# Attention in groups of four heads with one two-bank score tile, in a float32 decoder on one core

## The chip, the cores and the metric

The kernel runs on one core of one Trainium2 chip. The metric is the device time of one execution in microseconds. Three runs of the kernel before took 1315.48, 1319.79 and 1320.84 us; the median is 1319.79 us.

## The reference

A sequence of 256 tokens of width 1024 goes through two decoder layers and then through one layer of another kind. A decoder layer is a feed-forward block, a mixer and another feed-forward block. The mixer projects the normalized tokens and runs four attentions side by side, each of 256 columns, whose outputs are joined and multiplied by `w_out`:

```python
ya = neighbourhood_mixer(...)   # 4 heads of 64, additive bias per head
yb = mla_mixer(...)             # 4 heads of 96 (64 + 32 with rope), no bias
yc = diff_mixer(...)            # 4 heads, two maps of 32 each, additive bias
yd = gqa_mixer(...)             # 4 query heads of 64 on 2 key heads, no bias
x = x + jnp.concatenate([ya, yb, yc, yd], axis=-1) @ w_out[l]

# dense attention, per block of 128 queries
logits = einsum('bqhd,bkhd->bhqk', q, k) * scale (+ bias)
p = softmax(logits); y = einsum('bhqk,bkhd->bqhd', p, v)
# differential attention: two maps m per head, one value
p = softmax(logits)                       # b h m q k
w = p[:, :, 0] - lam * p[:, :, 1]
```

The last layer has 8 heads of causal attention over the 256 tokens (`moba`), 8 heads of causal attention in a window of 128 with a sink logit in the softmax (`swa`), a pooling branch, and gates. All weights and activations are float32.

## The kernel before, in words

TensorE (PE) is given every product twice or three times: each weight is staged from memory (`st`), rounded on ScalarE to `hi` and its rest `lo` formed on VectorE (`Weights.cut`, a unit of 1024 columns each), and `acc` (L339) issues three matmuls of 128 rows by up to 512 columns for one 128-row piece of it. These are the rows `mmps<-...` of the trace; the text calls them the weight matmuls. `proj` (L496) and `wide` (L521) loop over them. After each piece they call `tick` (L446), which runs pieces of other work that a small time model (`Clock`) takes to be ready: norms, rope, and the attentions, each written as a generator. So the attentions are dealt out between the weight matmuls, in an order that is fixed when the program is built. Each engine then works off its own queue in order.

An attention hands `softmax_pv` (L572) a list of jobs. Before the change a job is one block of 128 queries with two heads, or one differential head with its two maps. It has four steps:

- `scores` (L581): the products of queries and keys, for the two halves s = 0 and 1 of the job, into two score tiles of 256 columns in PSUM (`psS`, L321, trace name `sps`, one buffer each, each in a bank of its own). Where a bias is added VectorE writes score plus bias to `E` and takes its maximum in one instruction (trace name CUSTOM_DVE_ANT_0); else it takes the maximum alone (TENSOR_REDUCE, `nm<-sps`). ScalarE takes the exponential of each half with its sum (`E`). A differential job then combines its two maps on VectorE (`E<-E,cf`).
- `transposes` (L628): PE transposes `E` (128 by 128 each) into a tile `tps`, and ScalarE copies it to `PT`.
- `values` (L638): PE multiplies the values with `PT`. The outputs of the two halves lie in rows 0 to 63 and 64 to 127 of one `tps` tile; a differential job has one half only. ScalarE copies to `yt`.
- `finish` (L657): PE transposes `yt`, VectorE scales by the reciprocal of the sum into `y`. After the last job of a query block `post` norms and transposes `y` into `yT`, which `wide` needs for `w_out`.

The loop at the end of `softmax_pv` (L684 to L703) starts the scores of a job while up to two score steps are ahead of the transposes (`i1 - i2 < 2`), and allows two `PT` at once. There are 8 differential jobs and 4 of each other attention in a layer, and 8 each of `moba` and `swa`: 56 in all. `tps` has two buffers (L242) and serves all transposes of the kernel, `mmps` has four (L240).

The tags in `wk` have two buffers unless said otherwise, so there are two `E` tiles and two `PT` tiles.

Of the kernel before, what the change touches and what calls it, by code (L numbers as in the profile page):

```python
# [10 lines left out]
F = mybir.dt.float32  # L11
# [218 lines left out]
def decoder(ctx, tc, a, out):  # L230
# [10 lines left out]
    s_p = [pool(f"s{i}", 1, space=PSUM) for i in range(2)]  # L241
# [56 lines left out]

    def v3(ap, n):
        return ap.rearrange("p (k n) -> p k n", n=n)  # L300
# [20 lines left out]
    def psS(i):  # L321
        ps = s_p[i].tile([128, 256], F, tag="s", name="sps")
        clock.ring(f"s{i}", 1, ps)
        return ps
# [247 lines left out]
    def softmax_pv(jobs, post, scored=None, have_v=lambda: True):  # L572
# [3 lines left out]
        n = len(jobs)  # L576
        diff = "nlam" in jobs[0]
        ns = 1 if diff else 2
        E, PT, YT, yts = {}, {}, {}, {}

        def scores(i):  # L581
            jb = jobs[i]
            w = jb["nk"] * 128
            ps = [psS(s) for s in range(2)]
            e = E[i] = wk.tile([128, 2, 256], F, tag="E", name="E")
            for s in range(2):
                q, k = jb["qk"][s]
                if not isinstance(q, tuple):
                    mm(ps[s][:, :w], q, k, True, True)
                    continue  # L590
                mm(ps[s][:, :w], q[0], k[0], True, False)
                mm(ps[s][:, :w], q[0], k[1], False, False)
                mm(ps[s][:, :w], q[1], k[0], False, True)
            nm = stat.tile([128, 2], F, tag="nm", name="nm")
            if jb["bias"] is not None:
                mx = stat.tile([128, 2], F, tag="mx", name="mx")
                for s in range(2):
                    dve.tensor_tensor_reduce(
                        out=e[:, s, :w], in0=ps[s][:, :w], in1=jb["bias"][s], scale=1.0,
                        scalar=-3e38, op0=ALU.add, op1=ALU.max, accum_out=mx[:, s:s + 1])  # L600
                dve.tensor_scalar(nm, mx, -1.0, None, op0=ALU.mult)
                src = [e[:, s, :w] for s in range(2)]
            else:
                src = [ps[s][:, :w] for s in range(2)]
# [3 lines left out]
            if "nsink" in jb:  # L608
                dve.tensor_tensor(out=nm, in0=nm, in1=jb["nsink"], op=ALU.min)
                es = stat.tile([128, 2], F, tag="es", name="es")  # L610
                dve.tensor_tensor(out=es, in0=nm, in1=jb["nsink"], op=ALU.subtract)
                act.activation(out=es, in_=es, func=ACTF.Exp)
            sm = stat.tile([128, 2], F, tag="sm", name="sm")
            for s in range(2):
                act.activation(out=e[:, s, :w], in_=src[s], func=ACTF.Exp, bias=nm[:, s:s + 1],
                               accum_out=sm[:, s:s + 1])
            if "nsink" in jb:
                dve.tensor_tensor(out=sm, in0=sm, in1=es, op=ALU.add)
            rs = jb["rs"] = stat.tile([128, 2], F, tag="rs", name="rs", bufs=6)
            dve.reciprocal(out=rs, in_=sm)  # L620
            if diff:
                cf = stat.tile([128, 1], F, tag="cf", name="cf")
                dve.scalar_tensor_tensor(out=cf, in0=sm[:, 0:1], scalar=jb["nlam"],
                                         in1=rs[:, 1:2], op0=ALU.mult, op1=ALU.mult)
                dve.scalar_tensor_tensor(out=e[:, 0, :], in0=e[:, 1, :], scalar=cf,
                                         in1=e[:, 0, :], op0=ALU.mult, op1=ALU.add)

        def transposes(i):  # L628
            nk = jobs[i]["nk"]
            ps = psT().rearrange("p (s k q) -> p s k q", s=2, k=2)  # L630
            PT[i] = wk.tile([128, 2, 2, 128], F, tag="PT", name="PT")
            for s in range(ns):
                for k in range(nk):
                    T(ps[:, s, k, :], E[i][:, s, tok(k)])
            copy(0, PT[i][:, :ns, :nk, :], ps[:, :ns, :nk, :])
            del E[i]

        def values(i):  # L638
            jb = jobs[i]
            ps = psT()[:, :128]  # L640
            for s in range(ns):
                r = slice(64 * s, 64 * s + 64)
                for k in range(jb["nk"]):
                    mm(ps[r, :], jb["v"][s][k], PT[i][:, s, k, :], k == 0, k == jb["nk"] - 1)
            if diff and i % 2 == 0:
                yts[0] = wk.tile([128, 128], F, tag="yt", name="yt")
            elif not diff:
                yts[0] = wk.tile([128, 128], F, tag="yt", name="yt")
# [8 lines left out]
        def finish(i):  # L657
            if diff and i % 2 == 0:
                return
# [52 lines left out]
    def mixers(l, cols, rows, nlam, norm_out):  # L712
# [337 lines left out]
        w = []  # L1050
# [393 lines left out]
```

## Time and profile before

| | |
|---|---|
| median of three runs | 1319.79 us |
| the profiled execution | 1318.63 us |
| its span, first to last instruction | 1316.5 us |
| PE busy | 1291.3 us (98%) |
| VectorE (DVE) busy | 792.7 us (60%) |
| ScalarE (ACT) busy | 722.5 us (55%) |
| mean granted clock of PE | 0.995 |

Times in the trace count from the start of the span. The first layer's attentions lie at about 226 to 330 us, the second's at 747 to 850, those of the last layer at 1089 to 1163. A row of a PE timeline merges neighbouring instructions of one kind; matmuls overlap in their rows, so what a step takes from PE is read from its start to the start of the next row, not from its own duration. A float32 matmul shows as two rows, so "x4" for values in the trace is "x2" in the program's order.

### The profile page before, as it was taken

How to read it: one execution, taken by the hardware profiler on the slowest of the kernel's cores; microseconds unless marked ns; L12 is line 12 of the kernel's file. 1: busy time of each engine (PE TensorE's matmuls, PEld its weight loads, DVE VectorE, ACT ScalarE, POOL GpSimd, SP SyncE). 2: the span in 40 equal slices, each digit the busy share in tenths (PEclk: the TensorE clock that was granted, in tenths of full speed). 3: DMA queues.
4: the chain of work that ended last, by engine and by line, in shares of the span. 5: the costliest groups of instructions: out<-in, count | busy, mean ns of one | idle time of the engine just before them, and what ended most of it. 6: DMA issues, size and time to landing. Idle time of an engine off the chain costs nothing.

```text
span 1316.5 us, 17826 instructions
## 1 busy us (share of the span) xinstructions
PE 1291.3 (98%) x6514; PEld 1046.1 (79%) x6514; DVE 792.7 (60%) x1615; ACT 722.5 (55%) x1223; POOL 28.6 (2%) x44
## 2 busy tenths in 40 slices
PE   8999999999999999999999999999999999999997
PEld 7788888766788888788888876678888887678886
DVE  5655449895655544755545798565554565555475
ACT  6544437866644444644435676664444466566543
POOL 0000001000000000100000000000000000000000
PEclk9999999999999999999999998999999999999999
DMA  8766657432566665666665733156667474245652
GB/s 278 219 181 188 183 166 238 126 97 65 172 190 184 183 188 164 208 183 188 186 186 167 218 115 98 45 179 189 185 181 235 144 234 127 80 145 168 205 170 80
DMA packets 109815, 221.80 MB, mean 168 GB/s; under 512 B 7456, under 2 KB 30368, under 8 KB 109728
## 3 DMA queue, kind: packets, MB, share of 16 engines
q1 hardware_dynamic: 109152, 220.04, 55.5%
q8 instruction: 51, 0.84, 0.3%
q10 hardware_dynamic: 576, 0.63, 0.1%
q14 instruction: 36, 0.29, 0.1%
HBM read 219.59 MB, written 1.05 MB: 168 GB/s over the span
## 4 chain that ended last, share of the span: by engine, by line
PE 82%; DMA 6%; DVE 5%; ACT 4%; issue 1%; POOL 1%; SPq 0%; POOLq 0%; ACTq 0%; DVEq 0%
PE mmps L333 71%; PE tps L337 6%; PE sps L333 3%; DMA st<-in_w_in_dram 3%; PE tps L333 3%; DVE lo L154 2%; ACT hi L154 2%; DMA st<-in_ffn_w_gate_dram 2%; DMA st<-in_ffn_w_up_dram 1%; DVE xTl L153 1%; ACT junk L154 1%; ACT xTh L153 1%; POOL r L154 1%; DVE x L153 0%; DVE qkT L153 0%
## 5 line engine op out<-in xcount | busy, mean ns | idle before, releaser
L154 DVE TENSOR_TENSOR lo<-st,hi 128x1024 fp32r<-128x1024 f32 (+2 forms) x403 | 488.2, 1214 | 395.3 <-ACT hi L154 394.5
L154 ACT ACTIVATE hi<-st 128x1024 fp32r<-128x1024 f32 (+2 forms) x403 | 421.9, 1050 | 427.6 <-PE mmps L333 348.8
L333 PE MATMUL mmps<-hi,xTh 128*128 128x512 f32 (+2 forms) x1200 | 451.9, 377 | 1.0 <-ACT xTh L153 1.0
L333 PE MATMUL mmps<-hi,xTl 128*128 128x512 f32 (+2 forms) x1200 | 446.3, 372 | 0.0
L333 PE MATMUL mmps<-lo,xTh 128*128 128x512 f32 (+2 forms) x1200 | 446.2, 372 | 0.0
L333 PEld LDWEIGHTS mmps<-hi,xTh 128*128 128x128 f32 x1200 | 226.1, 188 | 42.4 <-issue 2.5
L333 PEld LDWEIGHTS mmps<-hi,xTl 128*128 128x128 f32 x1200 | 226.2, 188 | 38.2 <-issue 0.5
L333 PEld LDWEIGHTS mmps<-lo,xTh 128*128 128x128 f32 x1200 | 226.3, 189 | 36.2 <-issue 1.0
L333 PE MATMUL mmps<-lo,hTh 128*128 128x512 f32 x352 | 138.1, 392 | 0.0
L333 PE MATMUL mmps<-hi,hTh 128*128 128x512 f32 x352 | 137.8, 392 | 0.0
L333 PE MATMUL mmps<-hi,hTl 128*128 128x512 f32 x352 | 113.6, 389 | 0.0
L333 PE MATMUL mmps<-hi,yT 128*128 128x512 f32 (+1 forms) x248 | 89.0, 416 | 0.6 <-ACT yT L153 0.6
L333 PEld LDWEIGHTS mmps<-hi,hTl 128*128 128x128 f32 x352 | 66.1, 188 | 13.6
L333 PEld LDWEIGHTS mmps<-hi,hTh 128*128 128x128 f32 x352 | 66.1, 188 | 13.6
L333 PEld LDWEIGHTS mmps<-lo,hTh 128*128 128x128 f32 x352 | 66.1, 188 | 13.1
L154 POOL TENSOR_TENSOR r<-ms,mhalf 128x1 f32<-128x1 f32 x40 | 28.4, 711 | 1283.1 <-DVE ms L154 1283.0
L333 PEld LDWEIGHTS mmps<-hi,yT 128*128 128x128 f32 x248 | 46.1, 190 | 11.4 <-ACT yT L153 1.9
L333 PE MATMUL mmps<-lo,yT 128*128 128x512 f32 (+1 forms) x124 | 49.7, 401 | 0.0
L154 ACT ACTIVATE E<-E,nm 128x256 f32<-128x256 f32 (+1 forms) x80 | 38.3, 480 | 14.9 <-DVE nm L154 14.7
L153 ACT ACTIVATE fg<-mmps,r 128x512 f32<-128x512 f32 (+1 forms) x48 | 31.1, 652 | 21.7 <-PE mmps L333 21.7
L153 ACT ACTIVATE xTh<-tps,gains 128x128 fp32r<-128x128 f32 x112 | 31.6, 365 | 15.5 <-PE tps L337 15.5
L153 ACT ACTIVATE PT<-tps 128x512 f32<-128x512 f32 (+1 forms) x56 | 27.9, 502 | 21.4 <-PE tps L337 20.8
(172 smaller groups left out, 1035.0 us busy)
## 6 DMA issues: line engine op xcount, KB each, us to landing
st<-in_w_in_dram SPq DMA_DIRECT2D x90, 512.0 KB, 4.0
st<-in_ffn_w_up_dram SPq DMA_DIRECT2D x88, 512.0 KB, 4.0
st<-in_ffn_w_down_dram SPq DMA_DIRECT2D x88, 512.0 KB, 3.6
st<-in_ffn_w_gate_dram SPq DMA_DIRECT2D x87, 512.0 KB, 3.8
st<-in_w_out_dram SPq DMA_DIRECT2D x24, 512.0 KB, 3.7
st<-in_w_in_dram SPq DMA_DIRECT2D x8, 416.0 KB, 4.2
scratch<-in_t5b_dram SPq DMA_DIRECT2D x4, 512.0 KB, 5.1
scratch<-in_nab_dram SPq DMA_DIRECT2D x4, 512.0 KB, 7.3
```

The costliest lines, as they stand in the source:

```text
L153: return f(*args, **kw)
L154: return f(*args, **kw)
L333: nc.tensor.matmul(ps, lhsT=lhsT, rhs=rhs, start=start, stop=stop)
L337: nc.tensor.transpose(ps, src, ident)
```

## The change

A job becomes a group: four heads of one query block, as two pairs p = 0 and 1 of two halves s; for the differential attention two heads with both maps. There are 28 groups in place of 56 jobs. `psS` gives one tile of two banks, half s in bank s; the whole tile is one buffer. A group has two `E` tiles. Maxima of attentions without a bias are taken over both pairs at once, the small statistics have four columns, and a differential group multiplies the transposes of its two heads with their values into the two row halves of one tile. `PT` of the second pair is copied by VectorE. The loop lets a group's scores start only once the transposes of the group ahead have been issued (`i1 == i2`), and one group's `PT` at a time. Below is its core.

```diff
-    s_p = [pool(f"s{i}", 1, space=PSUM) for i in range(2)]
+    s_p = pool("s", 1, space=PSUM)
...
-        ps = s_p[i].tile([128, 256], F, tag="s", name="sps")
-        clock.ring(f"s{i}", 1, ps)
+        ps = s_p.tile([128, 2, 2, 256], F, tag="s", name="sps")
+        clock.ring("s", 1, ps)
...
         def scores(i):
...
+            ps = psS()
+            es = E[i] = [wk.tile([128, 2, 256], F, tag="E", name="E") for _ in range(2)]
+            for p in range(2):
                 for s in range(2):
...
+                    q, k = g["qk"][p][s]
+                    o = ps[:, s, p, :w]
...
+                    mm(o, q[0], k[0], True, False)
+                    mm(o, q[0], k[1], False, False)
+                    mm(o, q[1], k[0], False, True)
...
                 for s in range(2):
-                    dve.tensor_reduce(out=nm[:, s:s + 1], in_=src[s], axis=AX.X, op=ALU.max,
-                                      negate=True)
+                    dve.tensor_reduce(out=two(nm)[:, :, s], in_=ps[:, s, :, :w], axis=AX.X,
+                                      op=ALU.max, negate=True)
...
         def transposes(i):
...
+            if diff:
+                ps = psT().rearrange("p (s k q) -> p s k q", s=2, k=2)
+                pt = wk.tile([128, 2, 2, 128], F, tag="PT", name="PT")
+                for p in range(2):
+                    for k in range(nk):
+                        T(ps[:, p, k, :], E[i][p][:, 0, tok(k)])
+                copy(0, pt, ps)
+                PT[i] = [pt]
+            else:
+                for p in range(2):
...
+                    for s in range(2):
+                        for k in range(nk):
+                            T(ps[:, s, k, :], E[i][p][:, s, tok(k)])
+                    copy(p, pt[:, :, :nk, :], ps[:, :, :nk, :])
+                    PT[i].append(pt)
...
         def values(i):
...
+            w = 128 if diff else 256
+            ps = psT()[:, :w]
+            for p, pt in enumerate(PT[i]):
+                for s in range(2):
+                    v = g["v"][s] if diff else g["v"][p][s]
+                    for k in range(g["nk"]):
+                        mm(ps[64 * s:64 * s + 64, tok(p)], v[k], pt[:, s, k, :], k == 0,
+                           k == g["nk"] - 1)
...
-            elif i2 < i1 and att["pt"] < 2 and e_at[i2] <= now:
+            elif i2 < i1 and att["pt"] < 1 and e_at[i2] <= now:
...
-            elif i1 < n and i1 - i2 < 2 and (i1 == 0 or e_at[i1 - 1] <= now + 300):
+            elif i1 < n and i1 == i2:
...
             for t in range(2):
-                for h in range(4):
-                    rs = [slice(64 * (h % 2) + 32 * m, 64 * (h % 2) + 32 * m + 32)
-                          for m in range(2)]
+                for j in range(2):
+                    rs = [slice(64 * j + 32 * m, 64 * j + 32 * m + 32) for m in range(2)]
```

How this moves instructions is read from the order of the two built programs. Line 333 of the kernel before, where all matmuls are issued, is line 337 after, and the transposes' L337 is L341.

First, PE in the differential attention of layer 0, before: steps of one head (`sps` are scores, `tps<-ident,E` transposes, `tps<-PT,v` values) among the weight matmuls.

```order
L337 MATMUL tps<-ident,E 128x128 x2
L333 MATMUL sps<-qkT 128x256 x6
L333 MATMUL mmps<-hi,xTh 128x512
L333 MATMUL tps<-PT,v 64x128 x2
L333 MATMUL mmps<-lo,xTh 128x512
L333 MATMUL mmps<-hi,xTl 128x512
L337 MATMUL tps<-ident,yt 128x128
```

The same place after, with steps of two heads.

```order
L337 MATMUL sps<-qkT 128x256 x12
L337 MATMUL mmps<-hi,xTh 128x512
L341 MATMUL tps<-ident,E 128x128 x4
L337 MATMUL mmps<-lo,xTh 128x512
L337 MATMUL mmps<-hi,xTl 128x512
L337 MATMUL mmps<-hi,yT 128x384
L337 MATMUL mmps<-lo,yT 128x384
L337 MATMUL mmps<-hi,yT 128x384
L337 MATMUL tps<-PT,v 64x128 x4
```

Twelve score matmuls and four value matmuls stand in a row where six and two did; the weight matmuls between are the same in number over the attention.

Second, PE where the latent attention (`kT,qT` of 96 rows) begins in layer 0, before.

```order
L337 MATMUL tps<-ident,u 128x128 x8
L333 MATMUL sps<-kT,qT 128x256 x2
L333 MATMUL mmps<-hi,yT 128x512
L333 MATMUL sps<-kT,qT 128x256
L337 MATMUL tps<-ident,E 128x128 x2
L333 MATMUL sps<-kT,qT 128x256
L337 MATMUL tps<-ident,E 128x128 x2
L333 MATMUL sps<-kT,qT 128x256 x2
```

The same place after: the scores of the first group, then those of the second.

```order
L337 MATMUL sps<-kT,qT 128x256 x4
L337 MATMUL mmps<-hi,yT 128x512 x2
L337 MATMUL sps<-kT,qT 128x256 x2
L341 MATMUL tps<-ident,yn 128x128 x2
L341 MATMUL tps<-ident,u 128x128 x4
L337 MATMUL sps<-kT,qT 128x256
L337 MATMUL mmps<-hi,yT 128x512
```

And a little later after, from the values of the first group on into the neighbourhood attention (`qkT`).

```order
L337 MATMUL mmps<-hi,yT 128x512 x2
L337 MATMUL tps<-PT,v 64x128 x8
L341 MATMUL tps<-ident,E 128x128 x8
L337 MATMUL sps<-qkT 128x256 x3
L341 MATMUL tps<-ident,yt 128x128 x2
L337 MATMUL sps<-qkT 128x256 x9
L337 MATMUL tps<-PT,v 64x128 x8
L337 MATMUL sps<-qkT 128x256 x6
L341 MATMUL tps<-ident,E 128x128 x2
L337 MATMUL sps<-qkT 128x256 x2
L341 MATMUL tps<-ident,E 128x128 x2
L337 MATMUL sps<-qkT 128x256 x2
```

ScalarE's queue of that place after, from the exponentials of the first latent group to those of the second.

```order
L153 ACTIVATE E,sm<-sps,nm 128x256 x4
L153 ACTIVATE yT<-tps,gcol 128x2x128
L153 ACTIVATE qkT<-tps,qcol 128x2x128
L153 ACTIVATE qkT<-tps 128x2x128
L154 ACTIVATE hi<-st 128x1024
L153 ACTIVATE qkT<-tps,qcol 128x2x128
L153 ACTIVATE PT<-tps 128x512
L153 ACTIVATE qkT<-tps 128x2x128
L154 ACTIVATE hi<-st 128x1024
L153 ACTIVATE yt<-tps 128x256
L153 ACTIVATE E,sm<-sps,nm 128x256 x4
```

The second group's exponentials have moved behind the first group's `yt`, and its transposes stand directly behind the first group's values, with no weight matmul between.

Third, PE in the grouped-query attention of layer 0, before (scores `kT,qT`, values `PT,ug`).

```order
L333 MATMUL sps<-kT,qT 128x256 x3
L337 MATMUL tps<-ident,E 128x128 x2
L333 MATMUL mmps<-hi,yT 128x512
L333 MATMUL sps<-kT,qT 128x256 x3
L337 MATMUL tps<-ident,E 128x128 x2
L333 MATMUL mmps<-lo,yT 128x512
L333 MATMUL mmps<-hi,yT 128x512 x2
```

The same place after.

```order
L337 MATMUL sps<-kT,qT 128x256 x11
L341 MATMUL tps<-ident,E 128x128 x8
L337 MATMUL sps<-kT,qT 128x256 x3
L341 MATMUL tps<-ident,yn 128x128 x2
L337 MATMUL sps<-kT,qT 128x256 x3
L337 MATMUL tps<-PT,ug 64x128 x8
L337 MATMUL sps<-kT,qT 128x256 x6
L341 MATMUL tps<-ident,yt 128x128 x2
```

The transposes of a group stand directly behind its own scores, and no weight matmul lies between there and the group's output transposes.

## Rows read from the trace of the kernel before

**Rows 1.** The page: PE over the span, and its granted clock by slices.

```profile
PE 1291.3 (98%) x6514; PEld 1046.1 (79%) x6514; DVE 792.7 (60%) x1615; ACT 722.5 (55%) x1223; POOL 28.6 (2%) x44
...
PEclk9999999999999999999999998999999999999999
```

**Rows 2.** The page: shares of the chain of work that ended last.

```profile
PE 82%; DMA 6%; DVE 5%; ACT 4%; issue 1%; POOL 1%; SPq 0%; POOLq 0%; ACTq 0%; DVEq 0%
```

**Rows 3.** Stretches: us, busy time (instructions) of each engine, clock, DMA share, GB/s.

```profile
core 0: us, PE busy (x) PEld busy (x) DVE busy (x) ACT busy (x) POOL busy (x), PEclk, DMA share, GB/s
226.40:279.70 53.30, 52.77 (x308) 40.73 (x308) 45.54 (x178) 40.51 (x97) 2.10 (x2) 1.00 0.50 149
279.70:329.60 49.90, 47.06 (x296) 32.46 (x295) 34.30 (x148) 32.90 (x101) 2.74 (x5) 0.97 0.17 50
...
799.90:850.50 50.60, 47.63 (x291) 32.94 (x290) 34.31 (x147) 32.51 (x101) 2.74 (x5) 0.93 0.16 47
...
1088.70:1162.90 74.20, 74.00 (x456) 52.01 (x457) 39.98 (x155) 47.33 (x131) 0.00 (x0) 1.00 0.32 93
```

**Rows 4.** Timeline of PE, differential attention: start us, us, instruction.

```profile
248.11 0.40 PE L333 MATMUL mmps<-hi,xTl 128*128 128x512 f32 x1
248.44 0.65 PE L333 MATMUL tps<-PT,v 128*64 128x128 f32 x4
249.02 0.62 PE L333 MATMUL sps<-qkT 32*128 32x256 f32 x6
249.57 0.50 PE L333 MATMUL mmps<-hi,xTh 128*128 128x512 f32 x1
249.91 0.40 PE L333 MATMUL mmps<-lo,xTh 128*128 128x512 f32 x1
250.15 0.40 PE L333 MATMUL mmps<-hi,xTl 128*128 128x512 f32 x1
```

**Rows 5.** Timeline of PE: values of two heads, both row halves.

```profile
288.99 0.67 PE L333 MATMUL tps<-PT,v 128*64 128x128 f32 x8
289.58 0.50 PE L333 MATMUL mmps<-hi,yT 128*128 128x512 f32 x1
```

**Rows 6.** Timeline of PE: eight transposes.

```profile
308.24 1.03 PE L337 MATMUL tps<-ident,E 128*128 128x128 f32 x8
309.03 0.48 PE L333 MATMUL mmps<-hi,yT 128*128 128x512 f32 x1
```

**Rows 7.** Timeline of PE: the first latent scores, idle time before and its releaser.

```profile
279.79 1.03 PE L333 MATMUL sps<-kT,qT 96*128 96x256 f32 x4
280.46 0.59 PE L333 MATMUL mmps<-hi,yT 128*128 128x512 f32 x1
281.51 0.70 PE L333 MATMUL sps<-kT,qT 96*128 96x256 f32 x2 [0.46 <-ACT E L153]
```

**Rows 8.** Waits of PE from 279.7 to 329.6: total us, times, longest.

```profile
PE sps L333 <- ACT E L153: 2.3, 4, 1.1
```

**Rows 9.** Groups of instructions by shape, 226 to 343 us: busy us, mean ns.

```profile
L154 DVE TENSOR_REDUCE hss<-scratch 128x8 f32<-128x512 f32 x2 | 1.4, 680 | 0.0
```

**Rows 10.** The same of ScalarE.

```profile
L153 ACT ACTIVATE E<-sps,nm 128x256 f32<-128x256 f32 x16 | 7.5, 471 | 2.9 <-DVE nm L153 1.8 <-DVE r L154 1.2
L153 ACT ACTIVATE PT<-tps 128x512 f32<-128x512 f32 x12 | 7.1, 596 | 6.2 <-PE tps L337 6.1
```

**Rows 11.** Timeline of ScalarE: two exponentials of one job.

```profile
284.09 0.47 ACT L153 ACTIVATE E<-sps,nm 128x256 f32<-128x256 f32 x1
...
284.54 0.47 ACT L153 ACTIVATE E<-sps,nm 128x256 f32<-128x256 f32 x1
```

**Rows 12.** Timeline of VectorE: score plus bias with its maximum, twice.

```profile
300.17 0.42 DVE L153 CUSTOM_DVE_ANT_0 E<-sps,scratch 128x256 f32<-128x256 f32 x1
...
300.51 0.42 DVE L153 CUSTOM_DVE_ANT_0 E<-sps,scratch 128x256 f32<-128x256 f32 x1
```

**Rows 13.** Timeline of PE in the last layer: values of one job of 128 keys.

```profile
1094.92 0.44 PE L333 MATMUL tps<-PT,vm 128*64 128x128 f32 x4
1095.29 0.44 PE L337 MATMUL tps<-ident,E 128*128 128x128 f32 x2
```

More of the change, by code (lines that the diff above doesn't have):

```diff
@@ new lines, in scores @@
+            if "nsink" in g:
+                dve.tensor_tensor(out=two(nm), in0=two(nm), in1=g["nsink"], op=ALU.min)
+                ex = stat.tile([128, 4], F, tag="es", name="es")
+                dve.tensor_tensor(out=two(ex), in0=two(nm), in1=g["nsink"], op=ALU.subtract)
+                act.activation(out=ex, in_=ex, func=ACTF.Exp)
+            sm = stat.tile([128, 4], F, tag="sm", name="sm")
+            for p in range(2):
+                for s in range(2):
+                    e, c = es[p][:, s, :w], 2 * p + s
+                    act.activation(out=e, in_=e if g["bias"] is not None else ps[:, s, p, :w],
+                                   func=ACTF.Exp, bias=nm[:, c:c + 1], accum_out=sm[:, c:c + 1])
@@ L620, in scores @@
+            if "nsink" in g:
+                dve.tensor_tensor(out=sm, in0=sm, in1=ex, op=ALU.add)
+            rs = g["rs"] = stat.tile([128, 4], F, tag="rs", name="rs", bufs=6)
             dve.reciprocal(out=rs, in_=sm)
             if diff:
[L622 to L626, printed above, removed]
@@ L628, in transposes @@
-        def transposes(i):
[L629 to L635, printed above, removed]
+                cf = stat.tile([128, 2], F, tag="cf", name="cf")
+                dve.scalar_tensor_tensor(out=cf, in0=two(sm)[:, :, 0], scalar=g["nlam"],
+                                         in1=two(rs)[:, :, 1], op0=ALU.mult, op1=ALU.mult)
@@ L636, in transposes @@
             del E[i]
         def values(i):
[L639 to L648, printed above, removed]
@@ L655, in values @@
+            yt = YT[i] = wk.tile([128, 256], F, tag="yt", name="yt", bufs=1)[:, :w]
+            copy(0, yt, ps)
             del PT[i]
         def finish(i):
-            if diff and i % 2 == 0:
-                return
-            ps = psT()[:, :128]
-            T(ps, YT[i])
+            g, yt = groups[i], YT.pop(i)
+            w = yt.shape[1]
+            ps = psT()[:, :w]
+            for p in range(w // 128):
+                T(ps[:, tok(p)], yt[:, tok(p)])
             if diff:
-                for j in (i - 1, i):
-                    dve.tensor_scalar(jobs[j]["y"], ps[:, 64 * (j % 2):64 * (j % 2) + 64],
-                                      jobs[j]["rs"][:, 0:1], None, op0=ALU.mult)
-            else:
-                dve.tensor_tensor(out=jobs[i]["y"], in0=heads(ps),
-                                  in1=jobs[i]["rs"][:, :, None].to_broadcast([128, 2, 64]),
-                                  op=ALU.mult)
+                dve.tensor_tensor(out=g["y"], in0=heads(ps),
+                                  in1=two(g["rs"])[:, :, 0:1].to_broadcast([128, 2, 64]),
+                                  op=ALU.mult)
+            else:
+                dve.tensor_tensor(
+                    out=g["y"], in0=ps.rearrange("p (a b d) -> p a b d", a=2, b=2),
+                    in1=two(g["rs"])[:, :, :, None].to_broadcast([128, 2, 2, 64]), op=ALU.mult)
@@ L685, in softmax_pv @@
                 end = timed(finish, i4)
-                t = jobs[i4]["t"]
-                if post and (i4 == n - 1 or jobs[i4 + 1]["t"] != t):
+                t = groups[i4]["t"]
+                if post and (i4 == n - 1 or groups[i4 + 1]["t"] != t):
                     spawn(post(t), True, end)
```

167 lines of the change are left out of this document (83 added, 84 removed).

## Prediction

> **What bounds the kernel now.** I read the page's busy times and clock first [rows 1]: PE is busy 98% of the span at nearly full clock, DVE 60%, ACT 55%. The shares of the chain of work come next [rows 2]: PE 82%, DVE and ACT together 9%. So the change can bring only what it takes from PE's own queue, and can cost only what PE waits. Then I cut the span at the attentions [rows 3]. The differential phase of a layer (53.30 us) is full of PE work, 52.77, with DVE next at 45.54. The stretch of the three other attentions is the one place with slack: 49.90 us with PE busy 47.06 at clock 0.97 in layer 0, 50.60 with 47.63 at 0.93 in layer 1. The last layer's attention stretch is full: 74.00 of 74.20. Last I read step prices from PE's timelines, start to start [rows 4 to 7].
>
> The sums go against the profiled execution, 1318.63 us (a span of 1316.5 and 2.1 outside). The median of the runs, 1319.79, is 1.2 higher, and I add that at the end.
>
> **Prices.** A weight matmul directly behind another takes .24 (249.91 to 250.15); ahead of a step of another kind or behind it it takes about .33 (248.11 to 248.44, 249.57 to 249.91) [rows 4]. So each passage between weight matmuls and attention steps costs some .10. Values of one differential head take .58, scores of one job .55 for three matmuls a half [rows 4]. Values of two heads into both row halves take .59 [rows 5]: the second head is nearly free. Eight transposes take .79, .10 each [rows 6]. Two latent scores take .67 [rows 7]. So, from this, .09 to .11 for each score matmul of the other kinds.
>
> **Differential phase, per layer.** It has 8 jobs before, 4 groups after.
> - Values: 8 x .58 = 4.6 becomes 4 x .59 = 2.4: −2.3. This is the firm gain; nothing hides it, as PE is full there.
> - Scores: 8 x .55 = 4.4. A group has twelve, four halves that lie in the two banks. If a second pair runs beside the first as in the job, .88 (.55 and three more at .11); if not, 2 x .55 = 1.10. The first gives −.9, the second 0. The first is nearer, since the halves still alternate between banks; I take −.9.
> - Passages: about half the steps, so some 8 fewer stays between weight matmuls, .10 each: −.8.
> - Waits: a group's chain on the other engines is four adds with maximum, at .34 [rows 12], four exponentials at .45 [rows 11], the small statistics and two combinations: 6 to 7 us, against some 7 us of weight matmuls between its scores and its transposes. DVE is busy 85% of this stretch, so it will sometimes be late. From 0 to 1.5; I take +.7.
>
> Sum: −4.0 gross, −3.3 net per layer.
>
> **Latent, neighbourhood and grouped-query attention, per layer.** Here PE has few weight matmuls left, so steps stand against each other in the order. Counted from the first latent score to the last `yt` transpose, the order of the program has 56 weight matmuls of 512 columns and 16 transposes of other work before, 62 and 26 after. For equal content before is then 49.9 + 6 x .24 + 10 x .10 = 52.3 in layer 0 and 53.1 in layer 1 [rows 3], 52.7 in the mean.
>
> After, PE's work alone at full clock: 62 x .24 = 14.9; 8 latent scores x .335 = 2.7; 48 other scores x .10 = 4.8; 86 transposes x .10 = 8.6; values of 12 pairs x .59 = 7.1; 14 of the 16 stays between weight matmuls (two lie at the ends) x 2 passages x .10 = 2.8. Together 40.9. The same sum for before, with 23 stays in place of 16 (7 x .20 more), is 42.3, which leaves 52.7 − 42.3 = 10.4 of waits and lost clock there. Part of that the stretches show openly: 2.84 and 2.97 not busy, clock loss (1 − .97) x 49.9 = 1.5 and (1 − .93) x 50.6 = 3.5, 2.5 in the mean. Part sits inside the rows or between them, as the .46 ahead of the next latent scores, which wait for an exponential [rows 7].
>
> What is new is that one score tile serves all. The next group's first score waits until the last exponential (or the last add) of the group ahead has read it; before, four such waits cost 2.3 in layer 0, the longest 1.1 [rows 8]. What stands behind a waiting score on PE is all the rest, weight matmuls too. I walked the order with the prices above and these for the other engines: a reduction over two pairs .68 [rows 9], .45 per exponential [rows 11], .60 for a `PT` copy on ACT [rows 10] and .60 to .68 for the second on DVE, which no row shows (nearest: ACT's copy and the reduction of 512 elements).
> - Scores of the second latent group behind all four exponentials of the first: 2 x .68 + 4 x .45 less the weight matmuls issued between, 2.2 with the passage.
> - `PT` copies and the free `tps` buffer ahead of the values: .9.
> - Transposes of the second latent group, whose exponentials stand on ACT behind `yt`, with no weight matmul between: 1.7.
> - Scores of the second neighbourhood group behind four adds: .8.
> - A `tps` buffer behind the block's `yT`: 2.1.
> - Grouped-query transposes directly behind their own scores: 2.2, reductions and first exponentials.
> - Several under .4: 1.0.
>
> Sum 10.9; with the clock loss of before, 2.5, it is 13.4. The stretch comes to 40.9 + 13.4 = 54.3 against 52.7: +1.6 per layer. The bounds are wide: with waits as before (10.4 for 13.4) it is −1.4; with the whole chain of a group (2 x .68 + 4 x .45 + .60 = 3.8) exposed at four of six groups and the clock loss doubled, 40.9 + 15.2 + 5.0 = 61.1, +8.4. The clock is a price by itself: it fell in this stretch alone, the one in which PE waits [rows 3].
>
> [...]
>
> **Last layer.** Windowed jobs of 128 keys have values at .37 [rows 13], and the 16 jobs become 8 groups. Values in both row halves were there before, so less is to be had: −.9 on values, as two jobs' passages become one, +.3 on scores split by single transposes. The stays between weight matmuls are no fewer (34 and 35 in the order). The same single tile adds about 1.1 of waits among 132 weight matmuls. +.5, from −1 to +3.
>
> **Sum.** 2 x (−3.3 + 1.6) + .5 = −2.9: 1318.63 − 2.9 = 1315.7 for the profiled execution, 1316.9 beside the median. DMA and SP's queue stay as they are: the loads of weights keep their order, and no transfer is moved.
>
> **The rivals.**
> - Waits stay as they were. PE issues the other steps while the chain runs, the stretch is −1.4, the differential phase its full −4.0, the last layer −.6: 2 x −5.4 − .6 = −11.4, 1308.4. For it: PE is what everything waits for, and 10.4 is much already. Against: there is nothing to issue between a group's scores and its transposes in the grouped-query part.
> - It does not do what it says in the full phase: twelve scores at 1.10 (0 for −.9), and DVE, 85% busy, makes the groups late by all of the rest of 3.1. With the stretch at +1.6 and the last layer at +.5 that is +3.7, 1323.5. For it: the DVE's share; against it: the 7 us of weight matmuls between a group's scores and its transposes.
> - Slower: the single score tile exposes the chain, with the clock falling. At +8.4 a stretch, 2 x (−3.3 + 8.4) + .5 = +10.7, 1330.5. It decides from waits and clock loss of 40.9 to 56.0, which is 15.1 a stretch (+3.3, no change at all), and reaches the 0.5% point at about 18.3. For it: steps directly behind their own chain in the order of the grouped-query part, and [rows 8]. Against: half the score steps stand where the group ahead has long been exponentiated.
>
> **How the numbers follow.** A difference under 0.5% (6.6 us, so between 1313.2 and 1326.4) can hardly be told from none. Forecast .45, own range 1311 to 1322; waits as before .22; no gain in the full phase .17; slower .16. Faster by over 0.5%: a quarter of the forecast and nine tenths of the first rival, .31. Slower: nine tenths of the last and a quarter of the one before, .18, and a little of the forecast, .20. Same: the rest, .49. The range from 1305 to 1330 leaves out a tenth at each end: the first rival's better half by a little, and half of the slower one.
>
> **What would show it.** In the changed profile the differential phase should be some 50 us for the same content, its scores in rows of x12 at .88 (1.10 is the second rival) and values x8 at .59. The three attentions' stretch should show PE idle of about 5 to 8 us, most of it ended by an exponential on ACT ahead of scores or transposes, and a clock not under .93. If that idle time is under 4, the first rival is right; if over 12 or the clock is under .90, the last. The forecast is wrong in its reason if the differential phase does not shrink by 3 us, whatever the sum.

## The result: 0.5% slower, and the profile after

The changed kernel took 1325.60 us (median of 22 runs, 1321.41 to 1330.36), the kernel before beside it 1318.42 us. The ratio is 1.0051, 95% interval 1.0038 to 1.0064. The forecast was 1316.9, no change or a little faster.

The page of the changed kernel, busy times and the chain of work that ended last:

```profile
PE 1281.8 (97%) x6514; PEld 1048.2 (79%) x6514; DVE 795.2 (60%) x1543; ACT 707.7 (53%) x1163; POOL 26.9 (2%) x44
...
PE 76%; DVE 8%; ACT 7%; DMA 6%; issue 2%; POOL 1%; SPq 0%; POOLq 0%; ACTq 0%; DVEq 0%
```

PE is busy 9.5 us less than in [rows 1], and the chain leaves PE more often: 76% for 82%, DVE and ACT 15% for 9% [rows 2]. The stretches that answer to [rows 3], in the same columns (differential phase; the three attentions from the first latent score to the last `yt` transpose, in either layer; last layer):

```profile
core 0: us, PE busy (x) PEld busy (x) DVE busy (x) ACT busy (x) POOL busy (x), PEclk, DMA share, GB/s
226.90:278.40 51.50, 49.30 (x296) 39.28 (x297) 42.56 (x162) 39.15 (x89) 2.14 (x2) 0.97 0.47 142
278.40:337.70 59.30, 49.53 (x309) 36.02 (x308) 39.44 (x139) 30.70 (x91) 2.75 (x5) 0.91 0.17 52
...
804.50:863.60 59.10, 49.30 (x309) 35.90 (x308) 39.43 (x139) 30.69 (x91) 2.80 (x5) 0.91 0.17 51
...
1099.20:1170.00 70.80, 70.71 (x456) 53.23 (x456) 39.60 (x135) 42.23 (x110) 0.00 (x0) 1.00 0.30 96
```

The stretch of the three attentions has PE idle for 9.8 us where it was 2.84 and 2.97, and its clock is 0.91 where it was 0.97 and 0.93. Since the order puts six more weight matmuls into it, it is better compared between two weight matmuls that are the same in both, here the 1140th and the 1260th. That is this row before

```profile
272.40:344.40 72.00, 68.31 (x405) 48.65 (x405) 51.23 (x186) 49.30 (x140) 4.16 (x8) 0.98 0.28 85
```

and this one after

```profile
272.00:351.00 79.00, 67.80 (x401) 49.87 (x400) 55.38 (x182) 43.55 (x119) 3.85 (x7) 0.94 0.26 81
```

+7.1 us by the two starts. Set against each other in this way, the sections of the program give: differential phase 0.0 in both layers, the three attentions with the tail behind them +7.1 and +4.5, the last layer −3.6, all else −0.8. The two spans (1323.6 and 1316.5) differ by 7.1; the rest is rounding.

What PE waits for in the stretch of layer 0 (total us, times, longest), after:

```profile
PE sps L337 <- ACT E L153: 3.0, 1, 3.0
PE tps L341 <- ACT E L153: 3.0, 2, 2.0
PE sps L337 <- DVE mx L153: 0.9, 1, 0.9
PE mmps L337 <- ACT yT L153: 0.7, 1, 0.7
PE tps L341 <- DVE yn L154: 0.7, 1, 0.7
PE tps L341 <- DVE PT L153: 0.6, 1, 0.6
```

Before, the exponentials were waited for by four score steps, 2.3 in all [rows 8]. They are now waited for once for 3.0, by the second latent group's scores, and by transposes for another 3.0. In PE's timeline these are the rows with a number in brackets (start us, us, instruction, idle time before and its releaser):

```profile
283.83 1.13 PE L337 MATMUL sps<-kT,qT 96*128 96x256 f32 x4 [3.02 <-ACT E L153]
...
294.96 1.80 PE L341 MATMUL tps<-ident,E 128*128 128x128 f32 x8 [0.95 <-ACT E L153]
296.69 0.62 PE L337 MATMUL sps<-qkT 64*128 64x256 f32 x3
...
323.38 1.81 PE L341 MATMUL tps<-ident,E 128*128 128x128 f32 x8 [2.04 <-ACT E L153]
325.12 0.62 PE L337 MATMUL sps<-kT,qT 64*128 64x256 f32 x3
...
327.04 2.03 PE L337 MATMUL tps<-PT,ug 128*64 128x128 f32 x16
329.00 1.01 PE L337 MATMUL sps<-kT,qT 64*128 64x256 f32 x6
```

Two things make steps behind a wait slow here, and they have to be kept apart. The eight grouped-query transposes behind the wait at 323.38 take 1.74 from start to start, where eight took .79 [rows 6], but the granted clock is 1.00 there. They start in pairs about .46 apart (323.38, 323.84, 324.29, 324.75), each pair behind one of the four exponentials, which ScalarE starts at 322.76, 323.23, 323.68 and 324.13; the row merges such short pauses. The same holds at 294.96 (1.73). So each of these two waits is about .9 longer than its bracket says. The values of two pairs at 327.04 are another matter: they take 1.96, where the same step takes 1.08 elsewhere in this profile (307.46 to 308.54, at a clock of 1.00), and the granted clock is 0.50:

```profile
323.40:325.10 1.70, 1.65 (x8) 0.79 (x8) 0.18 (x1) 1.70 (x7) 0.00 (x0) 1.00 0.01 5
327.00:329.00 2.00, 2.00 (x18) 1.63 (x17) 0.05 (x1) 0.00 (x0) 0.00 (x0) 0.50 0.00 0
```

The clock is 0.52 in 285 to 288.5 and 0.50 in 326 to 332, and PE is busy all through both pieces (3.50 of 3.50 us and 6.00 of 6.00): it works slowly there, it does not wait. In stretches of 10 us, after:

```profile
280.00:290.00 10.00, 6.99 (x29) 5.38 (x28) 8.40 (x42) 4.52 (x13) 0.00 (x0) 0.83 0.19 61
290.00:300.00 10.00, 8.30 (x69) 5.60 (x67) 9.46 (x30) 6.07 (x18) 0.00 (x0) 1.00 0.35 106
...
320.00:330.00 10.00, 7.91 (x52) 5.31 (x51) 2.58 (x5) 3.19 (x11) 0.00 (x0) 0.80 0.18 55
```

### The profile page after: what moved, and what is told of

It is laid out like the page before. It is cut to its first block, busy times and chain, and to the rows that moved or that the text cites. A ratio compares the mean times of both kernels' runs of the same rounds, so it can differ in the third digit from the quotient of the medians.

```text
span 1323.6 us, 17699 instructions
## 1 busy us (share of the span) xinstructions
PE 1281.8 (97%) x6514; PEld 1048.2 (79%) x6514; DVE 795.2 (60%) x1543; ACT 707.7 (53%) x1163; POOL 26.9 (2%) x44
## 4 chain that ended last, share of the span: by engine, by line
PE 76%; DVE 8%; ACT 7%; DMA 6%; issue 2%; POOL 1%; SPq 0%; POOLq 0%; ACTq 0%; DVEq 0%
PE mmps L337 66%; PE tps L341 5%; DVE lo L154 3%; ACT hi L154 3%; PE sps L337 2%; PE tps L337 2%; DMA st<-in_ffn_w_gate_dram 2%; DMA st<-in_w_in_dram 2%; DMA st<-in_ffn_w_up_dram 1%; ACT E L154 1%; ACT junk L154 1%; ACT xTh L153 1%; DMA st<-in_w_out_dram 1%; DVE xTl L153 1%; POOL r L154 1%
## 5 line engine op out<-in xcount | busy, mean ns | idle before, releaser
L337 PE MATMUL mmps<-hi,xTh 128*128 128x512 f32 (+2 forms) x1200 | 451.3, 376 | 0.7 <-ACT xTh L153 0.5
L337 PE MATMUL mmps<-hi,xTl 128*128 128x512 f32 (+2 forms) x1200 | 447.8, 373 | 0.0
L337 PE MATMUL mmps<-lo,xTh 128*128 128x512 f32 (+2 forms) x1200 | 446.6, 372 | 0.0
L337 PEld LDWEIGHTS mmps<-hi,xTh 128*128 128x128 f32 x1200 | 226.6, 189 | 40.1 <-issue 1.5
L337 PEld LDWEIGHTS mmps<-hi,xTl 128*128 128x128 f32 x1200 | 226.6, 189 | 38.9 <-issue 0.9
L337 PEld LDWEIGHTS mmps<-lo,xTh 128*128 128x128 f32 x1200 | 226.7, 189 | 36.0 <-issue 0.2
L337 PE MATMUL mmps<-lo,hTh 128*128 128x512 f32 x352 | 138.1, 392 | 0.0
L337 PE MATMUL mmps<-hi,hTh 128*128 128x512 f32 x352 | 137.8, 392 | 0.0
L337 PE MATMUL mmps<-hi,hTl 128*128 128x512 f32 x352 | 113.6, 389 | 0.0
L337 PE MATMUL mmps<-hi,yT 128*128 128x512 f32 (+1 forms) x248 | 87.7, 413 | 2.3 <-ACT yT L153 2.3
L337 PEld LDWEIGHTS mmps<-hi,hTh 128*128 128x128 f32 x352 | 66.1, 188 | 13.7
L337 PEld LDWEIGHTS mmps<-hi,hTl 128*128 128x128 f32 x352 | 66.1, 188 | 13.6
L337 PEld LDWEIGHTS mmps<-lo,hTh 128*128 128x128 f32 x352 | 66.1, 188 | 13.1
L337 PEld LDWEIGHTS mmps<-hi,yT 128*128 128x128 f32 x248 | 48.0, 195 | 13.5 <-ACT yT L153 4.1
L337 PE MATMUL mmps<-lo,yT 128*128 128x512 f32 (+1 forms) x124 | 50.5, 407 | 0.0
L341 PE MATMUL tps<-ident,E 128*128 128x128 f32 x176 | 33.9, 285 | 8.0 <-ACT E L153 6.0
```

Source lines behind the costliest of these rows:

```text
L337: nc.tensor.matmul(ps, lhsT=lhsT, rhs=rhs, start=start, stop=stop)
L341: nc.tensor.transpose(ps, src, ident)
```

## Experiments

The measured clock and span of every run split a time in two: span x granted clock is taken as an estimate of the time at full clock (its waits included), and the rest as one of what the lower clock cost. It leans on the values above, 1.96 at 0.50 for 1.08 at 1.00, and holds as far as PE is at work while the clock is low. Medians over the runs of each kernel. The runs come from several chips, so each ratio below is to the kernel before on the same chip, and a difference of a microsecond or two between rows of the table is not clear of noise:

| kernel | us | clock | span x clock | lost to the clock |
|---|---|---|---|---|
| before | 1319.2 | 0.994 | 1309.3 | 7.9 |
| changed | 1325.6 | 0.9875 | 1306.2 | 16.5 |
| changed, again (e9) | 1326.4 | 0.986 | 1306.0 | 18.5 |
| before + small tile (e12) | 1316.4 | 0.9955 | 1308.2 | 5.9 |
| changed + small tile (e10) | 1322.5 | 0.988 | 1304.7 | 15.8 |
| longest wait filled (e5; e11 alike) | 1321.0 | 0.988 | 1303.1 | 15.8 |
| the other waits filled (e6) | 1315.0 | 0.9935 | 1304.3 | 8.5 |
| all filled (e4) | 1311.8 | 0.998 | 1305.9 | 2.6 |
| two score tiles (e3) | 1315.1 | 0.9935 | 1304.1 | 8.5 |
| two tiles, filled (e7) | 1311.6 | 0.9975 | 1306.8 | 3.3 |
| groups in diff. and last layer (e1) | 1317.6 | 0.9905 | 1304.1 | 12.5 |
| the same, filled (e8) | 1311.4 | 0.996 | 1304.6 | 5.2 |
| groups in the last layer (e2) | 1316.0 | 0.994 | 1305.8 | 7.9 |

**e1 and e2, the change in parts.** Both keep the old loop and jobs of two heads beside the groups. Both also give the groups two score tiles of one bank, as e3 does, so they are not parts of the change exactly as it stands:

```diff
-    def psS():
-        ps = s_p.tile([128, 2, 2, 256], F, tag="s", name="sps")
+    def psS(i):
+        ps = s_p[i].tile([128, 2, 256], F, tag="s", name="sps")
...
-            yield from softmax_pv(jobs, post_rms(y, "mla_beta", 2), ...)
+            yield from softmax_pairs(jobs, post_rms(y, "mla_beta", 2), ...)   # na, gqa too; e2: diff too
```

> Groups only in the differential attention and in the last layer; the latent, neighbourhood and grouped-query attentions go back to jobs of two heads, with the old loop (two one-bank score tiles serve both forms). Theory (the loss sits in the stretch of these three, where a group's chain of maxima, exponentials and copies lies open on PE, and the clock falls behind the waits): the about 11.4 us lost there in the two layers go, the last layer's gain stays, so some 1314 to 1315 us against 1318.4 before; the stretch from the first latent score to the last yt transpose back to 50 to 51 us with a clock of 0.93 to 0.97. Rival (the loss comes from the groups in the full phases, by the wait of the first differential scores and a DVE that is late): the time stays at 1321 or more.

Measured: 1317.64 us, ratio to before 0.9985 (0.9969 to 1.0001). The direction is the theory's, the size is not: 8 us less than changed, where 11.4 were expected, and the stretches are 53.60 and 54.30 us at 0.97 and 0.94, not 50 to 51. Against the kernel before, the sections of the three attentions are still 2.4 and 1.1 us longer. In e3, with the same score tiles and groups everywhere, they are 3.3 and 1.7 longer, so going back to jobs of two heads wins only .9 and .6 there. The last layer keeps its gain (−4.1); the differential phase shows −3.0 in layer 0 and −0.1, at clock 0.97, in layer 1.

> Groups only in the last layer; both decoder layers in jobs of two heads. Theory (the 3.7 us that the last layer wins are a saving of its own, fewer passages and a second pair of values and scores beside the first): 1314.7 us. Rival (the last layer wins only because its weights had more time to arrive during the loss ahead of it): no change, 1318.4.

Measured: 1316.00 us, 0.9977 (0.9961 to 0.9992). Span x clock is 3.5 lower at the same loss to the clock, and the last layer's section is 4.1 us shorter. In e3, which reaches that layer 0.8 us ahead of the kernel before and so has had no more time to load, it is 4.1 shorter too. The saving is its own; the rival falls.

**e3, two score tiles of one bank.**

```diff
-            ps = psS()
+            ps = [psS(s) for s in range(2)]
...
-                    o = ps[:, s, p, :w]
+                    o = ps[s][:, p, :w]
```

> All in groups as after the change, but the score tile is two tiles of one bank each, released apart. Theory (the whole chain lies open, the form of the tile matters little, since the last two exponentials read both banks): the second latent group's scores start at most one exponential earlier, 0.5 us per layer, 1324.5 us. Rival (the release of the whole tile is the cause): the waits of scores go by half or more, 1320 or less.

Measured: 1315.08 us, 0.9969 (0.9954 to 0.9983). My theory falls and the rival's signs come: the form of the tile matters. The wait of the second latent scores is 0.9 us for 3.0, though a new wait of 2.4 stands behind them:

```profile
PE tps L340 <- DVE q L154: 2.4, 1, 2.4
PE tps L340 <- ACT E L153: 1.4, 1, 1.4
PE sps L336 <- ACT E L153: 0.9, 1, 0.9
```

All in all PE is idle for 7.6 us of the stretch and not 9.8, and it is 3.9 us shorter, at a higher clock:

```profile
274.60:330.00 55.40, 47.81 (x310) 34.67 (x310) 39.09 (x139) 30.23 (x91) 2.83 (x5) 0.94 0.18 56
```

The second latent scores come 3.30 us after the first ones (274.67 to 277.97) and not 5.38. ScalarE shows how, in the changed kernel

```profile
281.85 0.47 ACT L153 ACTIVATE E<-sps,nm 128x256 f32<-128x256 f32 x1 [1.33 <-DVE nm L153]
```

and with two tiles:

```profile
276.89 0.47 ACT L153 ACTIVATE E<-sps,nm 128x256 f32<-128x256 f32 x1 [0.16 <-DVE nm L153]
...
277.36 0.47 ACT L153 ACTIVATE E<-sps,nm 128x256 f32<-128x256 f32 x1
```

The first exponential starts 2.22 us after the first score, for 3.40: it no longer waits for the maxima of both banks. And the scores follow the second exponential, not the fourth. I had counted one exponential, .45. What is not separated is the release itself from the order: the time model follows the tiles, so at 348 of PE's 6514 places another matmul stands than in the changed kernel (the four second latent scores follow each other directly, for instance). Some 5 us of the 10.5 are not the tile's, though: the differential phases gain 2.5 us each here, as they do in e10 without any change to the tile.

**e4, the waits filled.** Extra matmuls that add a product with zeros to an open weight accumulation.

```diff
+    def filler(n):
+        if opened[0] is not None:
+            for _ in range(n):
+                nc.tensor.matmul(opened[0][:, :128], lhsT=ident,
+                                 rhs=zf.to_broadcast([128, 128]), start=False, stop=False)
...
+            filler(fill.get(("s", i), 0))     # ahead of the second scores: latent 12, neighbourhood 4
+            filler(fill.get(("t", i), 0))     # latent: 4 ahead of the second transposes
...
+                with tc.issue_after(ins.ins):  # grouped-query: 9 behind the first group's scores
+                    filler(fill["a", i])
```

> The changed kernel with 29 extra small matmuls per layer in the three-attention stretch that add a product with zeros to an open weight accumulation, put ahead of the scores, values and transposes on which PE waits (12 ahead of the second latent scores, 8 around the values and transposes behind, 9 behind the grouped-query scores); the waits themselves are as long as before. Theory (about half of the loss is the clock that falls behind the waits): the granted clock of the stretch rises from 0.91 to 0.97 or more and the stretch falls by 2 to 4 us, so 1318 to 1322 us for 1325.6. Rival (the waits are all, the slow steps behind them have another cause): no change, or slower by the extra matmuls that do not fit, 1325 to 1330, and the transposes and values behind the waits stay at 1.7 to 2.0 us.

Measured: 1311.79 us, 0.9944 (0.9921 to 0.9966); 6 us below the expected range, of which 3.1 come with the small tile of zeros (e10, below). The extra matmuls sit in the wait and the next step comes no earlier for them; x24 in the trace are 12 in the program:

```profile
280.53 2.84 PE L350 MATMUL mmps<-zf,ident 128*128 128x128 f32 x24
283.71 1.13 PE L339 MATMUL sps<-kT,qT 96*128 96x256 f32 x4 [0.34 <-ACT E L153]
...
323.08 1.80 PE L343 MATMUL tps<-ident,E 128*128 128x128 f32 x8
324.82 0.62 PE L339 MATMUL sps<-kT,qT 64*128 64x256 f32 x3
...
326.28 1.15 PE L339 MATMUL tps<-PT,ug 128*64 128x128 f32 x16
327.35 0.63 PE L339 MATMUL sps<-kT,qT 64*128 64x256 f32 x6
```

The scores start 5.37 us after the first latent score (278.34), as they do in the changed kernel (283.83 after 278.45: 5.38). The wait itself costs what it did; what is won lies behind it. The grouped-query values take 1.07 (326.28 to 327.35) and not 1.96. The transposes ahead of them still take 1.74, as the rival had said, since they follow the exponentials as in the changed kernel; they have no part in what is won. The stretches are 55.70 and 55.00 us at 0.94 and 0.97: the clock still falls in either layer of this profile (in layer 0 to 0.66 in 300 to 310). PE's order is that of e10 but for three scores a layer, which stand ahead of four transposes. Span x clock is 1305.9, within 1.2 us of the same kernel without them (e10), and the clock's loss is 2.6 for 15.8.

**e5, e6 and e11, which wait.** e5 fills only the longest, e6 only the others; e11 is e5 once more.

> The changed kernel with only the 12 extra matmuls ahead of the second latent scores in each layer, the longest wait (3.0 us of idle time); the other waits stay empty. Theory (each wait pulls the clock down behind itself, so a share of the 13.9 us of clock loss goes with each that is filled): clock 0.990 to 0.994 and 1317 to 1321 us, between the changed kernel's 1325.6 and the 1311.8 with all filled. Rival (one empty wait in the stretch is enough, the clock falls all the same): 0.988 and 1324 to 1326 us.

> The other part of the same: the 17 extra matmuls at the shorter waits (values and transposes of the latent attention, the grouped-query transposes), none ahead of the second latent scores. Theory: the rest of the 13.9 us, so 1317 to 1321 us at 0.990 to 0.994, and the two parts add up to about the whole. Rival (only the longest wait lets the clock fall): no change, 1324 to 1326 us.

> The kernel with 12 extra matmuls ahead of the second latent scores alone, once more, for a second profile on the chip of these runs. Theory (this wait costs little clock beside the shorter ones, which come one after the other): again 1319 to 1322 us, its stretches as long as those of the changed kernel. Rival (the first was a mean of unlike executions): 1317 or 1325.

Measured: e5 1320.98 us (1.0017, 1.0003 to 1.0031), e11 1320.98 (1.0021, 0.9997 to 1.0046), e6 1315.03 (0.9974, 0.9960 to 0.9987). Held against e10, which has their small tile, e5 wins 1.5 us, e6 7.5 and e4 10.7; the 1.5 is not clear of noise, as the intervals of e5, e10 and e11 overlap. In the profile of e11 the sections of the three attentions are even longer than in the changed kernel, 82.1 and 81.0 us for 79.0 and 77.7. The parts don't add up and my theory of a share for each wait fails: filling the longest wait brought back next to nothing of the clock (0.988 for the whole run, as in e10). Its rows of 10 us show what happens instead. With the first wait filled (e5) the clock stays up behind it and falls further on, in stretches with open waits:

```profile
280.00:290.00 10.00, 9.36 (x60) 7.47 (x58) 9.56 (x42) 5.77 (x16) 0.00 (x0) 1.00 0.13 48
290.00:300.00 10.00, 8.82 (x59) 6.30 (x60) 8.25 (x36) 4.34 (x15) 0.55 (x1) 0.66 0.34 107
...
320.00:330.00 10.00, 7.92 (x48) 5.33 (x44) 2.58 (x5) 3.18 (x11) 0.00 (x0) 0.69 0.13 48
```

With the others filled (e6) it falls at the first, once more to 0.83 in 300 to 310, and stays up at the grouped-query transposes:

```profile
280.00:290.00 10.00, 8.73 (x33) 7.13 (x34) 7.11 (x36) 4.60 (x13) 0.00 (x0) 0.66 0.01 2
...
320.00:330.00 10.00, 9.95 (x78) 7.75 (x77) 4.21 (x8) 4.00 (x14) 0.00 (x0) 1.00 0.16 51
```

**e9, e10 and e12, controls.** e9 is the changed kernel again; e10 and e12 add the 128x1 tile of zeros and the instruction that sets it, and nothing else, to the changed kernel and to the one before.

> The changed kernel once more, for a second profile. In its first profile the differential phase had none of its gain (0.0 us per layer against the kernel before, clock 0.97), while the kernels with extra matmuls further on, whose order up to there is the same, gained 1.9 to 3.4 us there. Theory (a matter of the single execution: the first differential scores wait 0 to 1.4 us for their operand, and a long wait there pulls the clock down): 1324 to 1327 us, and the differential phase of one layer at least gains 2 us or more at clock 1.00. Rival (it is a property of the program): 0.0 in both layers again, with 0.97.

> The changed kernel with only the 128x1 tile of zeros, and the one instruction that sets it, of the kernels with extra matmuls: no extra matmul. Theory (the extra matmuls do it): 1324 to 1327 us and clock 0.985 to 0.989, as the changed kernel. Rival (the small tile moves addresses or the start, and that alone gave the 4.6 us or a part of the 13.8): 1321 us or less.

> The kernel before with the small tile of zeros alone. Theory (the 3.9 us that the tile gave the changed kernel are the two clock drops behind its first differential scores, which the kernel before does not have): no change, 1317 to 1321 us. Rival (the tile makes any such kernel faster): 1315 us or less, and then the kernels with extra matmuls must be held against this one.

Measured: e9 1326.40 us (1.0063, 1.0040 to 1.0087), with 0.97 and next to no gain (−0.5 and −0.3) in the differential phases again: there the rival holds, it is a property of this program. e10 1322.51 (1.0023, 1.0004 to 1.0043), between what the two expected: 3.1 less than the changed kernel, 3.9 less than e9 beside it. e12 1316.44 (0.9977, 0.9951 to 1.0004), again between: 3.5 less, but its interval reaches 1, so whether the tile helps the kernel before is open. With the tile on both sides the change costs 6.1 us, without it 6.4 (medians of the table).

In the changed kernel the first differential scores wait 1.40 us, and the clock falls behind them (stretches of 5 us):

```profile
227.67 0.38 PE L337 MATMUL sps<-qkT 32*128 32x256 f32 x1 [1.40 <-ACT qkT L153]
```

```profile
225.00:230.00 5.00, 3.60 (x27) 2.67 (x26) 4.06 (x10) 4.62 (x15) 2.14 (x2) 1.00 0.74 207
230.00:235.00 5.00, 5.00 (x20) 4.10 (x19) 3.60 (x13) 1.78 (x3) 0.00 (x0) 0.66 0.74 218
```

With the small tile (e10) PE comes to the same place with 0.17 us to wait, and the clock stays:

```profile
228.23 0.38 PE L339 MATMUL sps<-qkT 32*128 32x256 f32 x1 [0.17 <-ACT qkT L153]
```

```profile
225.00:230.00 5.00, 4.83 (x40) 4.08 (x38) 4.33 (x10) 5.00 (x16) 2.06 (x2) 1.00 0.59 150
230.00:235.00 5.00, 5.00 (x28) 4.11 (x26) 3.79 (x13) 2.69 (x5) 0.00 (x0) 1.00 0.86 270
```

The differential phase gains 2.7 us a layer there. Why one tile of 512 bytes shifts that wait is not settled; the order of PE's instructions is the same. Nor does the length of this wait alone decide what the clock does. In the second profile of the changed kernel (e9) the clock falls behind .78 (0.97 over the section; weight matmuls .43 apart from 230.23 on, .23 from 233.73 on); in e4 it stays at 1.00 in 230 to 235 behind .95; in layer 1 of the kernel before it stays at 1.00 behind 1.86. And in e12, the kernel before with the tile, the wait is 1.35, the clock falls to 0.70 in 230 to 235, and the section is 2.4 us longer, although the tile was thought to spare that kernel:

```profile
227.56 0.38 PE L337 MATMUL sps<-qkT 32*128 32x256 f32 x1 [0.78 <-ACT qkT L153]
...
228.86 0.38 PE L339 MATMUL sps<-qkT 32*128 32x256 f32 x1 [0.95 <-ACT qkT L153]
...
747.12 0.39 PE L333 MATMUL sps<-qkT 32*128 32x256 f32 x2 [1.86 <-ACT qkT L153]
...
227.66 0.38 PE L335 MATMUL sps<-qkT 32*128 32x256 f32 x2 [1.35 <-ACT qkT L153]
```

What is consistent is the program: in both profiles of the changed kernel the clock falls in the differential phase of either layer (0.97 over each section), and in the five profiles that add the small tile to it (e4, e5, e6, e10, e11) in neither (1.00).

**e7 and e8, towards the best version.** e7 is e3 with extra matmuls in the waits left; e8 is e1 with 15 around the second and third latent scores.

> Two one-bank score tiles and extra matmuls in the waits that are left (5 ahead of the second latent scores, 10 behind them, 5 around the latent values, 6 behind the grouped-query scores). Theory: span times granted clock, the time that PE would take at full clock, was 1304.5 us with two tiles; with the clock at 0.997 or more that is 1306 to 1310 us. Rival (the extra matmuls take as much time as they save, since shorter waits are filled): 1313 to 1316 us as with two tiles alone.

> Groups in the differential attention and the last layer, jobs of two heads in the three others, and 15 extra matmuls per layer in the waits around the second to third latent scores. Theory: span times clock was 1303.0 us for this form without them, its clock 0.9905; with the clock at 0.996 that is 1306 to 1311 us. Rival: no change, 1317.

Measured: e7 1311.61 us (0.9948, 0.9933 to 0.9963), e8 1311.44 (0.9950, 0.9927 to 0.9973), above the ranges by 1.6 and .4, but the rivals' 1313 and 1317 are not it. They are as fast as e4, and 4.8 and 5.0 us faster than before with the small tile. With the waits filled the form of the score tile no longer shows.

## Why the prediction was wrong

**The step that failed is the clock.** It was put as "with the clock loss of before, 2.5", while the same sum added more waits to that stretch. It is (1 − .91) x 59.3 = 5.3 there in either layer, and (1 − .97) x 51.5 = 1.5 in each differential phase, 13.6 for the 5.0 of before [rows 3]. Over the whole run, by the table, the clock's loss went from 7.9 to 16.5 us, +8.6; span x clock went from 1309.3 to 1306.2, −3.1, beside the forecast of −2.9. e4 shows it: with the first wait as long as in the changed kernel and PE kept at work in the waits the loss is 2.6 and the kernel is faster than before. The prediction's own sign fails too: the differential phase was to shrink by 3 us, and between the same weight matmuls it shrank by 0.0. The signs for the three attentions fell in between: idle 9.8 us (5 to 8 for the forecast, over 12 for the slower rival) and a clock of 0.91 (0.93 and 0.90). That the total at full clock came out is partly luck, since terms of both signs were off:

- **Values and scores of the differential phase: right.** In PE's timeline after, twelve scores take .92 (242.51 to 243.43), forecast .88, and values of two heads .60 (247.28 to 247.88), forecast .59:

```profile
242.51 0.98 PE L337 MATMUL sps<-qkT 32*128 32x256 f32 x12
243.43 0.50 PE L337 MATMUL mmps<-hi,xTh 128*128 128x512 f32 x1
...
247.28 0.67 PE L337 MATMUL tps<-PT,v 128*64 128x128 f32 x8
247.88 0.61 PE L337 MATMUL sps<-qkT 32*128 32x256 f32 x4
```

  The section's sums per layer, start to start, are 4.06 to 2.38 for values (within the same weight matmuls; seven heads before, eight after) and 5.17 to 4.38 for scores. The author's reason for .88, that the halves alternate between banks, was not tested: no run has both in one bank. The net −3.3 is −2.7 where the clock holds (1.00 in e10) and 0.0 in the changed kernel. The waits of +.7 were thought to be a late DVE; the one that stands there is the first score's on `qkT`, 1.40 for .45 before in layer 0 and 2.23 for 1.86 in layer 1, with the clock falling behind it (0.66 in 230 to 235 and in 755 to 760); the forecast had no fall of the clock in this phase.
- **The three attentions: right places, too small.** The waits stand where the walk of the order put them: 3.02 at the second latent scores (forecast 2.2 with the passage), .95 at the transposes behind (1.7), .92 at the second neighbourhood scores (.8), 2.04 at the grouped-query transposes (2.2). With the .9 that either row of transposes spends between exponentials, the second and the fourth are 1.9 and 3.0. The 2.1 forecast for a `tps` buffer behind `yT` did not come: the other waits of the list are .7 or less. The stretch is 59.3 and not 54.3: 18.4 of waits and lost clock, where 13.4 were forecast, 5.3 of it clock (for 2.5) and 13.1 waits (for 10.9). The slower rival gave 18.3 as the point of 0.5%. This stretch reached it; that the whole came out at 0.5% as well is chance, as the differential phases and the last layer were off in opposite directions.
- **The last layer: wrong sign.** Forecast +.5, measured −3.6. No wait came (70.71 of 70.80 us are busy; 1.1 was charged). And the claim that stays between weight matmuls are no fewer was wrong: over the same 190 weight matmuls PE leaves them 40 times before and 34 after, values stand in 9 places for 16. Weight matmuls take 42.53 for 44.76, values 6.80 for 7.71 (−.9, as forecast), scores 9.84 for 10.47. Six stays fewer at the prediction's .20 are 1.2 of the 2.2 on weight matmuls; the rest is not explained.

The waits of scores for exponentials in [rows 8] were weighed too lightly. In e3, as far as two tiles can be told from the order that they bring, the wait of the second latent scores goes from 3.0 to 0.9. The clock was lower behind waits in the changed kernel (0.66 in 230 to 235, 0.83 in 280 to 290), though not behind every wait (1.00 behind 1.86 in layer 1 of the kernel before). The clock should have been a term of the sum.

What is open: why the start of the differential phase waits longer in the program as changed, which waits let the clock fall and which do not, and how much of e12's 3.5 us is real.

## What to carry to other kernels

Where PE is the bound and its clock falls behind waits, as it did here (0.91 in the stretch with the added waits), count an added wait with two prices: its own length, and the steps behind it if the clock falls. Not every wait has the second price, but here it came to 8.6 us, for 3.1 won at full clock. Look at the granted clock of each stretch before and after, and at span x clock of each run, before looking for a mechanism. Before a buffer is merged with its neighbour, look at what is queued on PE behind the first writer of it. A row of transposes or values that is slow is not yet a sign of the clock (the transposes of 1.74 ran at 1.00): look whether it follows another engine step by step. And compare two programs with a control that adds an idle instruction, since one small tile alone moved the changed kernel by 3 to 4 us.

## What the runs showed of the hardware

- A wait of 1.40 us in a phase that is otherwise nearly full (49.30 of 51.50 us busy) was followed by 5 us at 0.66 (changed kernel); with 0.17 in the same place the clock stayed at 1.00 (e10). The length of one wait does not settle it: the clock fell behind .78 (e9) and stayed behind .95 (e4) and 1.86 (layer 1 of the kernel before).
- With one wait of 3.0 us filled (e5) the clock fell in the next 10 us and not by less: 0.83 and 1.00 in 280 to 290 and 290 to 300 (changed kernel) became 1.00 and 0.66.
- With 29 products with zeros a layer in the waits the granted clock of the whole run was 0.998 (e4), without them 0.988 (e10, medians).
- Eight transposes that follow four exponentials take 1.74 us at a clock of 1.00 (changed kernel and e4), where eight took .79.
